# Two memory pools move below the weight pools in a two-layer decoder trunk

## The chip, the cores and the metric

The kernel runs on one core of one Trainium2 chip. The metric is the device time of one execution in microseconds (us). Before the change the median of three runs is 618.76 us (618.07 to 618.80). TensorE is called PE, VectorE DVE, ScalarE ACT, GpSimd POOL, SyncE SP. The on-chip memory has 128 partitions; "address" below means the byte within a partition at which a tile begins, the same in all partitions.

## The reference

The input is x, 256 tokens by 1024 features in float32. Two residual layers follow one another, each a mixer of sixteen attention heads and a gated feed-forward part:

```python
h = rms_norm(x, ev_norm)                       # layer 0
mixed = even_mixer(h, w_in, ...)               # 8 forgetting heads, 8 stick-breaking heads, 64 wide
x = x + mixed @ ev_w_out                       # 1024 x 1024
g, u = split(rms_norm(x, ffn_norm[0]) @ w_gate_up, 2)   # 1024 x 5632
x = x + (silu(g) * u) @ w_down                 # 2816 x 1024
h = rms_norm(x, od_norm)                       # layer 1
mixed = odd_mixer(h, w_in, ...)                # 8 block-sparse heads with a bias, 8 latent heads
x = x + mixed @ od_w_out
# ... and the same gated part with the second weights
```

All is float32. The weights, some 100 MB in all, are read once.

## The kernel before

**Products.** A float32 product a·b is made of three faster ones: each operand is split into a rounded high part and the rest, and hi·hi, hi·lo and lo·hi are summed in an accumulator `acc`. For weights ACT writes the high part `whi` (L244) and DVE the rest `wlo` (L252); for the normed input the parts are `xh`, `xl`, for the heads' outputs `oh`, `ol`, for the feed-forward's hidden values `hh`, `hl`, for the latent rows `lath`, `latl`. In a product one operand is *stationary* (128 by 128, loaded into PE by LDWEIGHTS) and the other *moving* (128 by 256, 384, 416 or 512 columns, streamed through). In nearly all the stationary operand is a piece of `xh`, `xl`, `oh`, `ol`, `hh`, `hl`, `lath` or `latl` (the two token halves, 128 columns each) and the moving one a row block of `whi` or `wlo`. For the projections of the stick-breaking heads it is the other way round: `whi` or `wlo` is stationary and `xh` or `xl` moves (L593).

**Stages.** Input projections and attention of layer 0 (to about 118 us), output projection (to 134 us), gate-up products of the feed-forward (134 to 262 us; eleven pairs of 48 products, 512 columns wide), down products (262 to 320 us), then the same for layer 1: latent projection, 416 columns wide (320 to 330 us), mixer (to 427 us), output projection, gate-up (442 to 556 us), down products (to 613 us). In the last half of the last down products one token half is split into two blocks of 256 columns, so products of 512 and 256 columns alternate there.

**Weights.** SP loads pieces of up to 1 MB into four buffers `raw` (L203 to L221); a new load is issued when DVE has made the last piece of an older one. The split pieces are made ahead of their use by a planned clock (L256); that clock counts columns and knows no addresses. Buffers: four `raw`, three `whi`, three `wlo`, 8192 bytes per partition each.

**Memory.** Each pool takes a stretch of addresses; pools are stacked in the order in which they are opened (L288 to L293, then L425 and later), and every tile takes a multiple of 32 bytes. `const` holds constants, `xpool` the residual stream, `wraw` the raw weights, `wsp` the split weights, `actp` the tiles `xh`, `xl`, `oh`, `ol` (32 tiles of 1024 bytes), `small` squares, factors and other small rows. Above them stands a pool for one attention layer (`att0`, `att1`), which makes room for the feed-forward's pool (`ffn0`, `ffn1`, with `hh`, `hl`) and back. `const` holds one tile of 32 bytes that nothing uses (L452).

**Order.** A scheduler sets the order of each engine's instructions from priorities and from the clock above. PSUM has four accumulators and four other banks.

The addresses at which the tiles begin, and what is left of them on division by 256:

| tiles | address before | mod 256 | mod 512 |
|---|---|---|---|
| `raw` (4) | 44288, then every 8192 | 0 | 256 |
| `whi` (3) | 77312, ... | 0 | 0 |
| `wlo` (3) | 101888, ... | 0 | 0 |
| `xh`, `xl`, `oh`, `ol` | 126464 to 159232, every 1024 | 0 | 0 |
| `small` | 159232 to 166784 | | |
| `hh`, `hl` | 179072, 181120, ... every 2048 | 128 | 384 |
| `lath`, `latl` | 182656, ... every 1024 | 128 | 384 |
| `mob` (bias rows, loaded by POOL's queue) | 170880 | 128 | 384 |

Within a tile the pieces used begin at multiples of 512 bytes (token halves) or of the row block's length: 2048 bytes for 512 columns, 1024 for 256, 1664 for 416. So of the 416-wide row blocks every second begins at 128 mod 256 and the others at 0.

Of the kernel before, what the change touches and what calls it, by code (L numbers as in the profile page):

```python
# [281 lines left out]
def trunk_kernel(ctx: ExitStack, tc: tile.TileContext, x, ffn_norm, w_gate_up, w_down, rel_bias,  # L282
# [4 lines left out]
    nc = tc.nc  # L287
    const = ctx.enter_context(tc.tile_pool(name="const", bufs=1))  # L288
    xpool = ctx.enter_context(tc.tile_pool(name="xpool", bufs=2))
    wraw = ctx.enter_context(tc.tile_pool(name="wraw", bufs=4))  # L290
    wsp = ctx.enter_context(tc.tile_pool(name="wsp", bufs=3))
    actp = ctx.enter_context(tc.tile_pool(name="actp", bufs=2))
    small = ctx.enter_context(tc.tile_pool(name="small", bufs=2))  # L293
    psA = ctx.enter_context(tc.tile_pool(name="psA", bufs=4, space=bass.MemoryType.PSUM))
    psB = ctx.enter_context(tc.tile_pool(name="psB", bufs=4, space=bass.MemoryType.PSUM))
    dram = ctx.enter_context(tc.tile_pool(name="dram", bufs=1, space=bass.MemoryType.DRAM))
# [1205 lines left out]
```

## Time and profile before

| | |
|---|---|
| median of three runs | 618.76 us (618.07 to 618.80) |
| the profiled execution | 618.59 us; its span, first to last instruction, 616.6 us |
| granted clock of TensorE | 0.999 of 2.4 GHz |
| busy in the span | PE 607.8 us, DVE 397.1, ACT 334.0, POOL 20.1 |
| read from HBM | 104.41 MB, 174 GB/s over the span |

A busy PE is not a PE at its best: products follow each other at a distance of their own, and a product's recorded time includes some of the next one's. The distance between the starts of two products, read from the timeline, is what counts; where the timeline has two products in one row ("x2"), two distances lie between that row's start and the next one's.

### The profile page before, as it was taken

Reading aid. Unit: us, or ns where it says so; the run is one execution under the profiler, and the core shown is the slowest. Engines: PE = TensorE matmul, PEld = TensorE weight load, DVE = VectorE, ACT = ScalarE, POOL = GpSimd, SP = SyncE. Lnnn points to the kernel's source line nnn. Section 1 sums busy time; section 2 is a strip of 40 time slices with the busy share of each in tenths; the row PEclk is TensorE's granted clock in tenths of the full one; section 3 lists DMA queues with packets and bytes.
Section 4 is the critical chain, followed back from the end, with each engine's and each line's share of the span. In section 5 each row is a group of like instructions: output and inputs, shape, how many; then the busy total and the mean of one; then the engine's idle time right before and its main releaser. Section 6 shows DMA issues by size and latency. Waiting matters only on the chain.

```text
span 616.6 us, 8999 instructions
## 1 busy us (share of the span) xinstructions
PE 607.8 (99%) x3398; PEld 513.9 (83%) x3398; DVE 397.1 (64%) x847; ACT 334.0 (54%) x693; POOL 20.1 (3%) x50
## 2 busy tenths in 40 slices
PE   8999999999999999999999999999999999999997
PEld 7988898778888888888889988777888888888896
DVE  4898777476655655745446797976656665664541
ACT  6856666464544554535357676966544454453430
POOL 7200000010000000000000000000000000000000
PEclk9999999999999999999999999999999999999999
DMA  8954443449645645565558344054465465465400
GB/s 254 370 175 137 142 144 127 137 138 286 234 162 176 228 144 191 185 205 167 180 174 266 129 137 138 17 189 138 136 218 192 146 225 175 157 218 201 179 32 35
DMA packets 84204, 106.07 MB, mean 172 GB/s; under 512 B 3532, under 2 KB 69394, under 8 KB 84032
## 3 DMA queue, kind: packets, MB, share of 16 engines
q1 hardware_dynamic: 82880, 101.49, 49.7%
q0 software_dynamic: 1120, 3.86, 1.9%
q8 instruction: 27, 0.44, 0.3%
q14 instruction: 17, 0.14, 0.1%
q10 hardware_dynamic: 160, 0.14, 0.1%
HBM read 104.41 MB, written 3.17 MB: 174 GB/s over the span
## 4 chain that ended last, share of the span: by engine, by line
PE 87%; DVE 5%; DMA 3%; ACT 3%; issue 1%; SPq 1%; DVEq 0%; POOLq 0%; ACTq 0%
PE acc L113 77%; PE ps L113 10%; DVE wlo L113 2%; DMA raw<-in_ev_w_in 1%; ACT whi L113 1%; DMA x<-in_x 1%; DMA cbc<-cd 1%; DVE sm L113 1%; DMA cd<-cum 1%; DVE m L113 0%; DVE pm L113 0%; ACT pm L113 0%; SPq L438 0%; DVE qkn L113 0%; ACT sqh L113 0%
## 5 line engine op out<-in xcount | busy, mean ns | idle before, releaser
L113 DVE TENSOR_TENSOR wlo<-raw,whi 128x512 fp32r<-128x512 f32 (+3 forms) x300 | 236.4, 826 | 93.4 <-ACT whi L113 92.8
L113 ACT ACTIVATE whi<-raw 128x512 fp32r<-128x512 f32 (+3 forms) x300 | 204.6, 740 | 96.0 <-PE acc L113 92.0
L113 PE MATMUL acc<-whi,xh 128*128 128x512 f32 (+3 forms) x592 | 179.9, 355 | 0.0
L113 PE MATMUL acc<-whi,xl 128*128 128x512 f32 (+3 forms) x592 | 177.2, 350 | 0.0
L113 PE MATMUL acc<-wlo,xh 128*128 128x512 f32 (+3 forms) x592 | 177.1, 349 | 0.0
L113 PEld LDWEIGHTS acc<-whi,xl 128*128 128x128 f32 x592 | 111.8, 189 | 15.0 <-issue 1.0
L113 PEld LDWEIGHTS acc<-wlo,xh 128*128 128x128 f32 x592 | 111.9, 189 | 14.2 <-DVE wlo L113 0.2
L113 PEld LDWEIGHTS acc<-whi,xh 128*128 128x128 f32 x592 | 110.1, 189 | 13.9 <-issue 1.3
L113 PE MATMUL acc<-whi,hl 128*128 128x512 f32 (+1 forms) x198 | 60.5, 370 | 0.0
L113 PE MATMUL acc<-whi,hh 128*128 128x512 f32 (+1 forms) x198 | 60.4, 370 | 0.0
L113 PE MATMUL acc<-wlo,hh 128*128 128x512 f32 (+1 forms) x198 | 60.0, 369 | 0.0
L113 ACT ACTIVATE sg<-acc,rs 128x256 f32<-128x256 f32 x44 | 18.5, 471 | 69.0 <-PE acc L113 65.7
L113 DVE SCALAR_TENSOR_TENSOR t<-acc,rs,sg 128x256 f32<-128x256 f32 x44 | 19.3, 479 | 50.7 <-ACT sg L113 50.7
L113 PEld LDWEIGHTS acc<-wlo,hh 128*128 128x128 f32 x198 | 35.8, 188 | 6.8
L113 PEld LDWEIGHTS acc<-whi,hl 128*128 128x128 f32 x198 | 35.9, 188 | 6.7
L113 PEld LDWEIGHTS acc<-whi,hh 128*128 128x128 f32 x198 | 35.6, 188 | 6.7
L113 ACT ACTIVATE hh<-ps 128x512 fp32r<-128x512 f32 x22 | 13.2, 599 | 42.4 <-PE ps L113 42.4
L113 DVE TENSOR_TENSOR hl<-ps,hh 128x512 fp32r<-128x512 f32 x22 | 15.2, 692 | 20.4 <-ACT hh L113 20.4
L113 ACT ACTIVATE pm<-lg,sm 128x128 f32<-128x128 f32 (+1 forms) x48 | 21.4, 455 | 9.0 <-DVE sm L113 8.9
L113 PE MATMUL acc<-whi,oh 128*128 128x512 f32 x64 | 22.2, 410 | 0.0
L113 PE MATMUL acc<-wlo,oh 128*128 128x512 f32 x64 | 21.2, 400 | 0.0
L113 PE MATMUL acc<-whi,ol 128*128 128x512 f32 x64 | 20.3, 394 | 0.0
(179 smaller groups left out, 587.1 us busy)
## 6 DMA issues: line engine op xcount, KB each, us to landing
raw<-in_ffn_w_gate_up SPq DMA_DIRECT2D x44, 1024.0 KB, 5.8
raw<-in_ffn_w_down SPq DMA_DIRECT2D x20, 1024.0 KB, 4.9
raw<-in_ev_w_in SPq DMA_DIRECT2D x10, 1024.0 KB, 6.9
raw<-in_od_w_in SPq DMA_DIRECT2D x6, 1024.0 KB, 5.2
raw<-in_ev_w_out SPq DMA_DIRECT2D x4, 1024.0 KB, 4.8
raw<-in_od_w_out SPq DMA_DIRECT2D x4, 1024.0 KB, 4.8
brep<-bd POOLq DMA_DIRECT2D x1, 2048.0 KB, 9.1
raw<-in_ffn_w_down SPq DMA_DIRECT2D x4, 512.0 KB, 3.7
```

What stands on the lines that cost most here:

```text
L113: r = f(*a, **k)
```

## The change

The pools `actp` and `small` are opened before `wraw` and `wsp` instead of after them:

```diff
     xpool = ctx.enter_context(tc.tile_pool(name="xpool", bufs=2))
+    actp = ctx.enter_context(tc.tile_pool(name="actp", bufs=2))
+    small = ctx.enter_context(tc.tile_pool(name="small", bufs=2))
     wraw = ctx.enter_context(tc.tile_pool(name="wraw", bufs=4))
     wsp = ctx.enter_context(tc.tile_pool(name="wsp", bufs=3))
-    actp = ctx.enter_context(tc.tile_pool(name="actp", bufs=2))
-    small = ctx.enter_context(tc.tile_pool(name="small", bufs=2))
```

`raw`, `whi` and `wlo` go up by 40320 bytes (157 times 256, and 128 more); the tiles of `actp` and `small` go down by 82176 bytes (321 times 256). All other tiles stay where they were, the attention and feed-forward pools too, since the four pools together are as long as before. The instructions of every engine, their order and their waits are the same; in the built program the addresses differ and nothing else.

| tiles | address after | mod 256 | mod 512 |
|---|---|---|---|
| `xh`, `xl`, `oh`, `ol` | 44288 to 77056 | 0 | 256 |
| `small` | 77056 to 84608 | | |
| `raw` (4) | 84608, ... | 128 | 128 |
| `whi` (3) | 117632, ... | 128 | 384 |
| `wlo` (3) | 142208, ... | 128 | 384 |
| `hh`, `hl`, `lath`, `latl`, `mob` | as before | 128 | 384 |

## Rows read from the trace of the kernel before

**Rows 1.** The page: span, busy time and share of each engine.
```profile
span 616.6 us, 8999 instructions
PE 607.8 (99%) x3398; PEld 513.9 (83%) x3398; DVE 397.1 (64%) x847; ACT 334.0 (54%) x693; POOL 20.1 (3%) x50
```

**Rows 2.** The page: the chain that ended last, by engine.
```profile
PE 87%; DVE 5%; DMA 3%; ACT 3%; issue 1%; SPq 1%; DVEq 0%; POOLq 0%; ACTq 0%
```

**Rows 3.** Busy time by stretch: start:end, length, engines, clock, DMA share, GB/s.
```profile
14.00:29.00 15.00, 15.00 (x124) 14.59 (x123) 12.21 (x38) 13.84 (x36) 4.47 (x9) 1.00 1.08 371
...
147.00:262.00 115.00, 115.00 (x529) 95.10 (x528) 71.05 (x97) 55.44 (x78) 0.00 (x0) 1.00 0.58 195
```

**Rows 4.** Timeline of PE, gate-up: start, us, operation.
```profile
200.22 0.62 PE L113 MATMUL acc<-whi,xh 128*128 128x512 f32 x2
...
202.94 0.62 PE L113 MATMUL acc<-whi,xh 128*128 128x512 f32 x2
```

**Rows 5.** Timeline of PE, output projection of layer 0.
```profile
121.34 0.62 PE L113 MATMUL acc<-whi,oh 128*128 128x512 f32 x2
...
123.61 0.61 PE L113 MATMUL acc<-whi,ol 128*128 128x512 f32 x2
```

**Rows 6.** Timeline of PE, down products of layer 0, both halves.
```profile
274.25 0.63 PE L113 MATMUL acc<-whi,hh 128*128 128x512 f32 x2
...
276.58 0.63 PE L113 MATMUL acc<-whi,hl 128*128 128x512 f32 x2
...
305.93 0.63 PE L113 MATMUL acc<-whi,hh 128*128 128x512 f32 x2
...
308.72 0.62 PE L113 MATMUL acc<-whi,hh 128*128 128x512 f32 x2
```

**Rows 7.** Timeline of PE, last down products, 512 and 256 columns in turn.
```profile
586.24 0.28 PE L113 MATMUL acc<-whi,hh 128*128 128x256 f32 x1
...
587.64 0.28 PE L113 MATMUL acc<-whi,hh 128*128 128x256 f32 x1
```

**Rows 8.** Timeline of PE, latent projection, 416 columns.
```profile
326.46 0.54 PE L113 MATMUL acc<-whi,xh 128*128 128x416 f32 x2
...
327.59 0.53 PE L113 MATMUL acc<-whi,xh 128*128 128x416 f32 x2
...
328.72 0.54 PE L113 MATMUL acc<-whi,xh 128*128 128x416 f32 x2
```

**Rows 9.** Timeline of PE, a projection of layer 0, 256 columns.
```profile
19.73 0.28 PE L113 MATMUL acc<-whi,xl 128*128 128x256 f32 x1
...
20.93 0.28 PE L113 MATMUL acc<-whi,xh 128*128 128x256 f32 x1
```

**Rows 10.** PE's groups by shape: operation, count, busy us, mean ns, idle.
```profile
L113 PE MATMUL acc<-whi,xh 128*128 128x512 f32 x352 | 110.6, 395 | 0.0
...
L113 PE MATMUL acc<-whi,xh 128*128 128x256 f32 x208 | 60.2, 290 | 0.0
...
L113 PE MATMUL acc<-whi,hl 128*128 128x512 f32 x154 | 51.5, 396 | 0.0
...
L113 PE MATMUL acc<-whi,oh 128*128 128x512 f32 x64 | 22.2, 410 | 0.0
...
L113 PE MATMUL acc<-xh,whi 128*128 128x256 f32 x64 | 19.1, 299 | 0.0
```

**Rows 11.** DVE's groups by shape: a target at 0, then one at 128.
```profile
L113 DVE TENSOR_TENSOR wlo<-raw,whi 128x512 fp32r<-128x512 f32 x190 | 122.5, 684 | 53.5 <-ACT whi L113 53.3
...
L113 DVE TENSOR_TENSOR qkn<-acc,sm 128x512 f32<-128x512 f32 x8 | 5.5, 685 | 0.3
```

**Rows 12.** Waits over the run: who for whom, us, times, longest.
```profile
ACT whi L113 <- DMA raw<-in_ev_w_in: 1.9, 2, 1.0
```

**Rows 13.** The page: the weights' DMA queue, packets, MB, share of 16 engines.
```profile
q1 hardware_dynamic: 82880, 101.49, 49.7%
```

**Rows 14.** DMA queues from 320 to 329 us: the queue that loads `mob`.
```profile
q0 software_dynamic: 272, 1.05, 32.2%
```

## The prediction

> **What bounds the kernel now.** Read in this order: the busy times, the chain that ended last, the stretches, and then, because the first three leave only one engine, the distances between products in PE's timeline. PE is busy 99% of the span [rows 1] and 87% of the chain [rows 2]; over the 115 us of gate-up it is busy 115.00 us, while DVE has 71.05, ACT 55.44 and the DMA engines a share of 0.58 [rows 3]. So a stretch gets longer or shorter only if PE's products follow each other at another distance, or if something slower than PE appears.
>
> The distances are where the reader must look closely, since the same product of 512 columns takes two values. Gate-up: from 200.22 to 202.94 us lie 12 products, 226.7 ns each [rows 4]. Output projection: from 121.34 to 123.61 lie 10, 227.0 ns [rows 5]. Down: 10 products from 274.25 to 276.58, 233.0 ns, and 12 from 305.93 to 308.72, 232.5 ns [rows 6]. The columns, the number of stationary columns, the accumulators and the `whi`/`wlo` buffers are alike, and the output projection's weights come in pieces of 512 columns as the down weights do. What differs is where the stationary tile lies: `xh`, `xl`, `oh`, `ol` begin at 0 mod 256, as `whi` and `wlo` do; `hh` and `hl` begin at 128. The excess is 232.75 - 226.7 = about 6.0 ns, 2.7%. So PE's pace does hang on addresses, or on something that goes with them, and this change alters nothing but addresses.
>
> **The change part by part.** Nothing is added, removed or put in another order, on SP's and POOL's queues either, and no wait is added. What changes is mod 256: `raw`, `whi`, `wlo` go from 0 to 128; `xh`, `xl`, `oh`, `ol` stay at 0; `hh`, `hl`, `lath`, `latl` stay at 128. Before, the two operands of a product stand alike in gate-up and the output projections and unlike in the down products; afterwards it is the reverse.
>
> *512 columns, operands that come to stand unlike.* The groups by shape give 352 for one of three products with `xh` and 64 for one of three with `oh` [rows 10]: 3 x (352 + 64) = 1248. No row of before has the moving operand at 128 and the stationary one at 0 at this width. The bounds: nothing, from the latent projection, whose six products on a row block at 128 take 1.13 us (326.46 to 327.59) and whose next six, on a block at 0, take 1.13 us as well [rows 8]; or 6.0 ns, from the down rows [rows 6]. I take 6.0, the row of the same width: 416 columns are 1664 bytes, so one end of each latent block stands off 256 either way and the pair is no clean test. 1248 x 6.0 ns = 7.5 us, ends 0 and 7.5.
>
> *512 columns, operands that come to stand alike.* 154 x 3 = 462 products with `hh` or `hl` [rows 10], of which 66 are in the last half where 512 and 256 columns alternate. There, nine products (three of 512, six of 256) take 1.40 us [rows 7], and by the distances of gate-up and of a 256-wide projection, 120 ns [rows 9], they would take 3 x 226.7 + 6 x 120 = 1400 ns: no excess to win. The other 396 may win 6.0 ns: -2.4 us, ends -2.4 and 0.
>
> *256 columns.* 3 x (208 + 64) = 816 products, in 192 of them the weights are stationary [rows 10]. Their distance is 120 ns now [rows 9]. Bounds from the rows above: the mixed stretch, where six 256-wide products unlike in place cost nothing [rows 7], or half of the 512-wide excess, 3.0 ns (2.4 us). I take 0, the row of the same width; the ends are 0 and +2.4 us. The few 264-, 384- and 416-wide products, some 120, go the same way and are under 0.5 us.
>
> *DVE and ACT.* They write and read at other places, but a DVE result at 128 takes 685 ns for 512 columns and one at 0 takes 684 [rows 11]: nothing, and what it could be is covered by PE, since DVE is free 38% of gate-up [rows 3].
>
> *The loads.* `raw` moves to 128 mod 256. The bias rows `mob` are loaded to an address at 128 already: 1.05 MB take 32.2% of 16 engines for 9 us, 46.4 us of engine time or 44 us per MB [rows 14]; the weights at 0 take 49.7% of 16 x 616.6 us for 101.49 MB, 48 us per MB [rows 13]. So no price shows; I take 0. What would be exposed are the first 30 us, where the DMA engines are saturated (share 1.08, 371 GB/s) [rows 3]; ACT waits 1.9 us for them now, in two waits [rows 12]. In the feed-forward the share of 0.58 is cover enough. A rule speaks against this part: the Trainium skill, "DMA: Bandwidth & Descriptors", section "How a descriptor splits into AXI transactions", has a descriptor that doesn't start at a multiple of 256 bytes begin at the boundary below and pay for the bytes before. It says so of reads; if it held for writes into the on-chip memory too, a 1024-byte row would pay 1152 bytes' worth, by my estimate from that page 12.5% more in the saturated 15 us, +1.9 us at most. The `mob` row disagrees, and the sum goes without it.
>
> *Sum.* 7.5 - 2.4 + 0 = +5.1 us on the profiled execution's own 618.59 us (span 616.6 and 2 us around it): 623.7 us. That execution is 0.17 us below the median of the three runs, which is less than a measurement of this kernel can tell (about 0.2%, 1.2 us).
>
> **The rivals.**
> *A, each operand pays for itself:* a product slows when either operand is off 256. Then gate-up pays 7.5 us and the down products win nothing: 626.1 us, up to 628.5 with the 256-wide. For it: the down rows fit it as well as they fit "unlike". Against: the latent blocks at 128 and 0 read the same.
>
> *B, the place of the moving operand doesn't matter,* only that of the stationary one, or the feed-forward tiles' region. All 512-wide stationary tiles keep their remainder; only the 192 products with stationary weights could change, within 0.6 us. 618.6 us. For it: the latent projection, six products at 1.13 us twice [rows 8]. Against: half of it is untested, since before no 512-wide product had its moving operand off 256; whether remainder or region slows `hh`, no row tells. The Trainium skill, "SBUF — State Buffer", section "Who interferes with whom", goes further: PE's reads of the moving and of the stationary operand are independent and PE waits on nobody, by which no address should matter and the time stays at 618.6; the two values of the distance in rows 4 and 6 are hard to square with it.
>
> *C, faster:* the slow case is only a stationary tile at 128 against a moving one at 0, and the opposite case is free, as in the latent rows. Then the down products win 2.4 us and gate-up pays nothing: 616.2 us. It decides against my forecast as soon as the 1248 products pay less than 2.4 us / 1248 = 1.9 ns each.
>
> *D, the loads pay* after all, in the first 30 us, with B otherwise: the two waits of 1.9 us double, 620.5 us.
>
> **How the numbers follow.** Forecast 0.42, A 0.12, B 0.20, C 0.20, D 0.06. Faster by over 0.2%: C, 0.20. Slower by over 0.2%: forecast, A and D, 0.60, less some small sizes of the forecast's excess (half of it gives +1.4 us after the gain): 0.56. Within: 0.24. The range runs from just under C (616.0) to A with part of the 256-wide products (627.0); the forecast's own, with 3 to 6 ns per product and 0 to 2.4 us for the narrow ones, is 620 to 626.
>
> **What would show it.** Gate-up and output projections at about 233 ns per product (a pair of eleven 0.3 us longer, the eleven pairs of a layer 3.2 us), down products at about 227: the forecast. Both at 233: A. All as before: B. Gate-up at 227 and down at 227: C. The 256-wide projections tell their own price against 120 ns. For D the waits on `raw` in the first 30 us would grow while PE's distances stay. The forecast is wrong if gate-up keeps 226.7 ns.

## The result and the profile after

The changed kernel takes 623.34 us (median of 4 runs, 623.24 to 624.02) against 618.64 us (618.07 to 618.80): a ratio of 1.008, 95% interval 1.0062 to 1.0097. It is slower by 4.7 us; 623.7 was forecast. Of the executions behind the medians below, one of alike_again (3418.71 us) is left out.

The page of the changed kernel's profiled execution (624.02 us), to be held against [rows 1]: the busy times of DVE, ACT and POOL are within 0.8 us of before, PE's is 6.4 us longer (its weight loads', PEld, 2.3 us) with the same number of instructions.

```profile
span 622.1 us, 8999 instructions
PE 614.2 (99%) x3398; PEld 516.2 (83%) x3398; DVE 397.7 (64%) x847; ACT 334.8 (54%) x693; POOL 20.0 (3%) x50
```

Now the distances, as in [rows 4 to 7]. First the timeline of PE in gate-up: seven rows of two products lie between the two starts, so 14 distances in 3.27 us, 233.6 ns, where before there were 226.7.

```profile
200.30 0.63 PE L113 MATMUL acc<-whi,xh 128*128 128x512 f32 x2
...
203.57 0.63 PE L113 MATMUL acc<-wlo,xh 128*128 128x512 f32 x2
```

The same view of the output projection (10 distances in 2.31 us: 231 ns, before 227.0), of the down products (10 in 2.27 us: 227 ns, before 233), and of the last half, where three products of 512 and six of 256 columns take turns (nine in 1.42 us, before 1.40):

```profile
122.19 0.62 PE L113 MATMUL acc<-whi,ol 128*128 128x512 f32 x2
...
124.50 0.64 PE L113 MATMUL acc<-wlo,oh 128*128 128x512 f32 x2
...
278.08 0.62 PE L113 MATMUL acc<-whi,hh 128*128 128x512 f32 x2
...
280.35 0.62 PE L113 MATMUL acc<-whi,hl 128*128 128x512 f32 x2
...
590.24 0.51 PE L113 MATMUL acc<-whi,hh 128*128 128x512 f32 x2
...
591.66 0.51 PE L113 MATMUL acc<-whi,hh 128*128 128x512 f32 x2
```

Where products of 512 columns follow one another, what was fast has become slow and the reverse: the slow ones are again those whose two operands differ mod 256. The 256-wide products of the projections come to stand unlike and get a little faster: 12 distances in 1.42 us, 118.3 ns, where there were 120 [rows 9].

```profile
19.81 0.28 PE L113 MATMUL acc<-whi,xh 128*128 128x256 f32 x1
...
21.23 0.28 PE L113 MATMUL acc<-whi,xh 128*128 128x256 f32 x1
```

The stages, from the start of the first product of one stage to that of the next (both read in the timelines, in us):

| stage | before | after | |
|---|---|---|---|
| first 256-wide projection to the first gate-up product | 116.65 | 118.01 | +1.36 |
| gate-up, layer 0 (with the last part of the output projection) | 125.42 | 128.20 | +2.78 |
| down, layer 0 | 63.10 | 61.77 | -1.33 |
| latent projection and mixer of layer 1 | 105.52 | 105.46 | -0.06 |
| gate-up, layer 1 | 125.63 | 128.50 | +2.87 |
| down, layer 1, first half | 31.35 | 30.68 | -0.67 |
| down, layer 1, last half (512 and 256 in turn) | 30.36 | 30.86 | +0.50 |

The first line of the table isn't PE's pace alone. The busy times by stretch of the changed kernel (columns as in [rows 3]) show the loads at 338 GB/s between 14 and 29 us, where they were at 371, and a granted clock of 0.93 in the next stretch:

```profile
14.00:29.00 15.00, 14.91 (x122) 14.35 (x121) 11.03 (x30) 12.64 (x34) 4.42 (x9) 1.00 1.10 338
29.00:53.00 24.00, 22.43 (x174) 21.09 (x174) 23.30 (x89) 14.89 (x42) 1.12 (x2) 0.93 0.50 161
```

The waits of the first 53 us go with it: ACT waits for `raw` 3.1 us in four waits (before 1.9 in two, [rows 12]), the chain behind it is late, and PE sits idle 1.6 us at its end (0.3 us before). Right behind that idle time, from 34.1 us on, the records show a clock of 1.2 GHz for 3.4 us.

```profile
ACT whi L113 <- DMA raw<-in_ev_w_in: 3.1, 4, 1.8
...
PE ps L113 <- DVE sm L113: 1.6, 1, 1.6
```

Of the four executions only this profiled one has the fall of the clock: the three other runs took 623.24 to 623.36 us at a clock of 1.0. So the stages of the profiled executions differ by 5.45 us in all, and the medians by 4.7.

### The profile page after: what moved, and what is told of

Its sections match the earlier page's. It is cut to its first block, busy times and chain, and to the rows that moved or that the text cites. A ratio compares the mean times of both kernels' runs of the same rounds, so it can differ in the third digit from the quotient of the medians.

```text
span 622.1 us, 8999 instructions
## 1 busy us (share of the span) xinstructions
PE 614.2 (99%) x3398; PEld 516.2 (83%) x3398; DVE 397.7 (64%) x847; ACT 334.8 (54%) x693; POOL 20.0 (3%) x50
## 4 chain that ended last, share of the span: by engine, by line
PE 88%; DVE 5%; ACT 3%; DMA 2%; issue 1%; SPq 1%; ACTq 0%
PE acc L113 78%; PE ps L113 10%; DVE wlo L113 2%; DMA raw<-in_ev_w_in 1%; ACT whi L113 1%; DMA x<-in_x 1%; DVE sm L113 1%; DVE m L113 1%; DVE pm L113 0%; DVE lg L113 0%; ACT pm L113 0%; SPq L438 0%; ACT sqh L113 0%; ACT sq L113 0%; DVE qkn L113 0%
## 5 line engine op out<-in xcount | busy, mean ns | idle before, releaser
L113 PE MATMUL acc<-whi,xh 128*128 128x512 f32 (+3 forms) x592 | 181.8, 357 | 0.0
L113 PE MATMUL acc<-wlo,xh 128*128 128x512 f32 (+3 forms) x592 | 179.3, 353 | 0.1
L113 PE MATMUL acc<-whi,xl 128*128 128x512 f32 (+3 forms) x592 | 179.3, 353 | 0.0
```

What stands on the lines that cost most here:

```text
L113: r = f(*a, **k)
```

## The experiments

**Theory 1:** the distance between products follows from the difference of the two operands' addresses mod 256. **Theory 2:** the order of the pools matters in another way (which region, which neighbours). **Theory 3:** a load to an address off 256 is slower where the DMA engines are saturated. The first four kernels below run the same instructions in the same order; they differ in unused bytes, and alike_above has the pools in the order of before.

*alike_below*: the changed kernel with a gap that brings the weights, and with them the pools above, to 0 mod 256.

```diff
     small = ctx.enter_context(tc.tile_pool(name="small", bufs=2))
+    pada = ctx.enter_context(tc.tile_pool(name="pada", bufs=1)); pada.tile([P, 32], F32, name="gapa")
     wraw = ctx.enter_context(tc.tile_pool(name="wraw", bufs=4))
```

> The pools in the order of the changed kernel, with 128 unused bytes between small and wraw: raw, whi, wlo and the feed-forward's hh, hl all begin at 0 mod 256, as xh and xl do. Theory 1 (the difference of the two operands' remainders mod 256 sets the distance of products): gate-up 226.7 ns, down 227 ns, so the time is that of before less the 1.4 us that the down products won in the changed kernel, 617.2 us. Theory 2 (not the remainder but the order of the pools, that is which tiles lie below which): gate-up stays at 233 ns and the time at 623.3 us.

616.94 us (6 runs, 616.80 to 617.61); against before 0.9974 (0.9963 to 0.9986). The timeline of PE, gate-up and then down: 12 distances in 2.72 us and 10 in 2.27, 226.7 and 227 ns. 128 bytes take back the whole loss and win more; theory 2 forecast 233 ns and 623.3 us here, and falls.

```profile
199.96 0.62 PE L113 MATMUL acc<-whi,xh 128*128 128x512 f32 x2
...
202.68 0.62 PE L113 MATMUL acc<-whi,xh 128*128 128x512 f32 x2
...
280.40 0.62 PE L113 MATMUL acc<-whi,hh 128*128 128x512 f32 x2
...
282.67 0.62 PE L113 MATMUL acc<-whi,hl 128*128 128x512 f32 x2
```

*alike_above*: the same gap above `small` in the order of before, so that only the attention and feed-forward pools move.

```diff
     small = ctx.enter_context(tc.tile_pool(name="small", bufs=2))
+    pada = ctx.enter_context(tc.tile_pool(name="pada", bufs=1)); pada.tile([P, 32], F32, name="gapa")
     psA = ctx.enter_context(...)
```

> The pools in the order of the kernel before, with 128 unused bytes above small: only the attention and feed-forward pools move, hh and hl to 0 mod 256. Theory 1: down products at 227 instead of 233 ns, gate-up stays at 226.7, 617.2 us, the same as with the pools in the other order. Theory 2: nothing changes, 618.6 us.

617.06 us (7 runs), 0.9978 (0.9967 to 0.9990): the same as alike_below with the other order. Once the remainders agree, the order of the pools is worth nothing that these runs can tell.

*raw_off*: as alike_below, with the gap between `wraw` and `wsp`: only `raw` is at 128. *raw_even*: as the changed kernel, with 128 unused bytes below `wraw` and above it: `raw` alone is at 0.

```diff
 # raw_off
     wraw = ctx.enter_context(tc.tile_pool(name="wraw", bufs=4))
+    pada = ctx.enter_context(tc.tile_pool(name="pada", bufs=1)); pada.tile([P, 32], F32, name="gapa")
     wsp = ctx.enter_context(tc.tile_pool(name="wsp", bufs=3))
```

> As alike_below, but the 128 unused bytes lie between wraw and wsp, so only raw begins at 128 mod 256; every pair of operands in PE is alike. Theory 1 alone: as alike_below, 617.2 us. Theory 3 (a load to 128 mod 256 takes the DMA engines longer per packet where they are saturated, 338 instead of 371 GB/s between 14 and 29 us): PE's distances as in alike_below, the first 30 us late by 0.4 to 1.2 us, 617.6 to 618.4 us.

> As the changed kernel, but raw begins at 0 mod 256 while whi, wlo, hh and hl stay at 128 (128 unused bytes below wraw and 128 above it). Theory 1 alone: gate-up 233, down 227 ns, 623.3 us. With theory 3: the same distances, 371 GB/s between 14 and 29 us, 622.1 to 622.9 us.

raw_off takes 617.96 us (11 runs), 1.0 us more than alike_below on the same chip. The single runs tell two prices apart: in five of the eleven the granted clock was 0.996 or 0.997, median 618.73 us, and in the other six at least 0.999, median 617.73; alike_below's six all had 1.0. So the loads cost 0.8 us, and 1.0 us more where the clock falls. raw_even takes 622.58 us (5 runs, 622.05 to 622.80), 0.8 us less than the changed kernel, whose four runs (623.24 to 624.02) were taken at another time. Busy times of 14 to 29 us, raw_off first and raw_even behind it: the loads' rate, the last number, follows `raw` alone.

```profile
14.00:29.00 15.00, 14.94 (x123) 14.52 (x122) 10.61 (x29) 12.19 (x33) 4.41 (x9) 1.00 1.10 339
```

```profile
14.00:29.00 15.00, 15.00 (x126) 14.72 (x125) 12.33 (x40) 13.83 (x36) 4.22 (x9) 1.00 1.07 371
```

raw_off's profile has the wait of PE (2.0 us) and the fallen clock (0.93 from 29 to 53 us) too; in raw_even's the same wait is 0.4 us and the clock stays at 1.00.

```profile
PE ps L113 <- DVE sm L113: 2.0, 1, 2.0
```

*sweep*: the distance measured by itself, in one execution at a granted clock of 1.0. The core of this new kernel, shortened, is

```python
def group(n, m, s):                      # m, s in elements past a multiple of 256 bytes
    for kt in range(8):
        for w, h in ((whi, xh), (wlo, xh), (whi, xl)):
            for tok in range(2):
                nc.tensor.matmul(a[tok][:, :n], h[:, s + 256 * kt + 128 * tok:][:, :128],
                                 w[:, m + 512 * kt:][:, :n], start=..., stop=...)
```

> Leaves out the whole model: TensorE alone runs groups of 48 products like those of gate-up (eight row blocks, three products each, two token halves), and each group has its own remainders mod 256 of the moving (m) and the stationary (s) operand; the output is filled with ones. Theory 1 (the difference m - s mod 256 decides): 512 columns at m = s take 226.7 ns a product whatever m is (0, 32, 64, 128), m - s = 128 takes 233 both ways (m 128, s 0 and m 0, s 128), and m 256 or s 256 are like 0. Its grain isn't known: if only multiples of 256 count, every other difference is slow; if the grain is 128, then 32 and 64 are something between. Rival (each operand's own remainder): m = s = 128 would be slow too. Rival (mod 512): m 256, s 0 would be slow. 256 columns: 120 ns alike and 117 to 120 unlike, as the kernels' traces show; 384 columns: 173.3 ns alike (columns plus 32 cycles of 2.4 GHz) and some 175.5 at 128.

The timeline of PE, the first row of a group and that of the next; n, m and s (bytes) stand in the accumulator's name. A group has 48 products, so the difference of two starts divided by 48 is the distance.

```profile
38.58 0.39 PE L70 MATMUL n512m0s0x<-whi,xh 128*128 128x512 f32 x1
49.46 0.63 PE L70 MATMUL n512m32s0x<-whi,xh 128*128 128x512 f32 x2
60.67 0.40 PE L70 MATMUL n512m64s0x<-whi,xh 128*128 128x512 f32 x1
71.66 0.63 PE L70 MATMUL n512m96s0x<-whi,xh 128*128 128x512 f32 x2
82.88 0.40 PE L70 MATMUL n512m128s0x<-whi,xh 128*128 128x512 f32 x1
94.07 0.40 PE L70 MATMUL n512m160s0x<-whi,xh 128*128 128x512 f32 x1
105.31 0.62 PE L70 MATMUL n512m192s0x<-whi,xh 128*128 128x512 f32 x2
116.51 0.40 PE L70 MATMUL n512m224s0x<-whi,xh 128*128 128x512 f32 x1
...
161.32 0.63 PE L70 MATMUL n512m0s128x<-whi,xh 128*128 128x512 f32 x2
172.48 0.40 PE L70 MATMUL n512m0s160x<-whi,xh 128*128 128x512 f32 x1
183.68 0.40 PE L70 MATMUL n512m0s192x<-whi,xh 128*128 128x512 f32 x1
194.68 0.40 PE L70 MATMUL n512m0s224x<-whi,xh 128*128 128x512 f32 x1
205.87 0.39 PE L70 MATMUL n512m128s128x<-whi,xh 128*128 128x512 f32 x1
216.76 0.62 PE L70 MATMUL n512m64s64x<-whi,xh 128*128 128x512 f32 x2
...
249.77 0.40 PE L70 MATMUL n512m256s0x<-whi,xh 128*128 128x512 f32 x1
260.70 0.62 PE L70 MATMUL n512m0s256x<-whi,xh 128*128 128x512 f32 x2
...
282.77 0.39 PE L70 MATMUL n512m16s0x<-whi,xh 128*128 128x512 f32 x1
293.89 0.40 PE L70 MATMUL n256m0s0x<-whi,xh 128*128 128x256 f32 x2
299.64 0.40 PE L70 MATMUL n256m32s0x<-whi,xh 128*128 128x256 f32 x2
305.30 0.40 PE L70 MATMUL n256m64s0x<-whi,xh 128*128 128x256 f32 x2
310.96 0.40 PE L70 MATMUL n256m96s0x<-whi,xh 128*128 128x256 f32 x2
316.70 0.40 PE L70 MATMUL n256m128s0x<-whi,xh 128*128 128x256 f32 x2
322.40 0.40 PE L70 MATMUL n256m160s0x<-whi,xh 128*128 128x256 f32 x2
...
386.95 0.55 PE L70 MATMUL n416m0s0x<-whi,xh 128*128 128x416 f32 x2
...
396.00 0.33 PE L70 MATMUL n128m0s0x<-whi,xh 128*128 128x128 f32 x2
```

With 512 columns: alike 226.7 ns (10.88 us), 32 off 233.5, 64 off 229.0, 96 off 233.8, 128 off 233.1. The other operand moved: 128 off 232.5, 192 (which is a difference of 64 again) 229.2. Both moved by 128: 226.9. Moved by 256: 227.7. The moving one 192 off pays in full, 233.3, so 64 and 192 aren't alike. At 512 columns, then, only the difference counts, moving minus stationary, mod 256, and theory 1 holds in the strong form; its grain is not 128 but finer, since 16 bytes already cost 5 ns (231.7). With 256 columns the sign turns: alike 119.8 ns, 32 or 64 off 117.9, 96 off 119.6, 128 off, which is the changed kernel's case, 118.7.

*loads*: theory 3 by itself, in one execution. SP alone loads 84 pieces of 1 MB.

> Leaves out the whole model: SP alone loads 84 pieces of 1 MB as gate-up's, rows of 1024 bytes, into four buffers, twelve pieces each at the remainders 0, 0, 128, 64, 32, 192 and 0 mod 256; the output is filled with weights. Theory 3 in the strong form (a row that doesn't start at a multiple of 256 takes one more piece of 256 bytes on its way): all remainders but 0 slow alike, from some 370 to some 338 GB/s, a median packet of 51 instead of 46 ns. Rival (only halves of 256, or only parts of 64 bytes, count): 128 slow and 64 not, or 32 slower than 64. Rival (the price in the whole kernels came from the other traffic of the first 30 us): 128 as fast as 0.

Busy times by stretch (length, POOL, clock, DMA share, GB/s), of stretches with the remainder 0, then 128 and 64, then 64 and 32, then 32 and 192:

```profile
20.00:55.00 35.00, 0.00 (x0) 1.00 1.09 386
...
90.00:125.00 35.00, 0.00 (x0) 1.00 1.10 348
125.00:160.00 35.00, 0.00 (x0) 1.00 1.10 348
160.00:195.00 35.00, 0.00 (x0) 1.00 1.09 348
```

386 GB/s at a multiple of 256 and 348 at every other remainder tried. A packet of 1024 bytes takes 46.0 ns on average at 0 and 51.2 to 51.7 ns off it, 11 to 12% more, at 32 as at 192. In the whole kernels the price shows where the DMA engines are saturated: from 14 to 29 us the median packet of 1024 bytes takes 46 ns before and 51 in the changed kernel, over the whole run 46 in both.

*apart64*: can the turned sign be used? As alike_below, but the split weights of the 256-wide projections lie 64 bytes further within their buffers, while all 512-wide products stay alike.

```diff
-        t = t[:, :un["n"]]
+        c = 16 if un["shape"][1:] == (256,) else 0; t = t[:, c:c + un["n"]]
...
-                un[t] = self.split_pool.tile([P, 2048], R32, name=f"w{t}{u}", tag=f"w{t}", bufs=3)
+                un[t] = self.split_pool.tile([P, 2112], R32, name=f"w{t}{u}", tag=f"w{t}", bufs=3)
...
-            self.rbc = small.tile([P, 256], F32, name=nm("rbc"), tag="rbc")
+            self.rbc = small.tile([P, 256], F32, name=nm("rbc"), tag="rbc", bufs=1)
```

> As alike_below, but in the 256-wide projections the weights lie 64 bytes further, so their 816 products have operands 64 (624 of them) or 192 apart mod 256, while all 512-wide products stay alike. The split weights' buffers grow by 256 bytes each and a row of factors has one buffer instead of two to make room; the order of instructions is the same. Theory 1 with the sweep's numbers (256 columns: 120.0 ns alike, 117.8 ns at 64 or 192): 816 x 2.2 ns = 1.8 us less than alike_below, 615.2 us. Rival: between transposes and attention products the 256-wide ones are too often interrupted for the distance to settle, or the stretch waits for attention anyway: 0 to 0.5 us less, 616.5 to 617 us.

> alike_below once more, on the chip of apart64, to compare it with: 616.9 us by every theory.

615.90 us (5 runs, 615.17 to 616.32), 0.9954 (0.9943 to 0.9966) against before; alike_again on the same chip 617.16 us (eight runs, 616.06 to 617.92), 0.9977 (0.9967 to 0.9987). The gain of 1.3 us lies between the 1.8 of the sweep, 615.2 us, and the 0.5 of the rival. The timeline of PE in a 256-wide projection: 10 distances in 1.18 us, 118 ns instead of 120 [rows 9].

```profile
19.50 0.28 PE L113 MATMUL acc<-whi,xh 128*128 128x256 f32 x1
...
20.68 0.28 PE L113 MATMUL acc<-wlo,xh 128*128 128x256 f32 x1
```

The products with stationary weights, whose operands stand 192 apart here, gain more: 10 distances in 1.14 us, 114 ns, where alike_below has 120. The sweep's group at 192, in which the moving operand was moved, has 117.8. So at 256 columns the difference alone does not give the pace; what else does was not tried.

```profile
57.15 0.28 PE L113 MATMUL acc<-xh,wlo 128*128 128x256 f32 x1
...
58.29 0.28 PE L113 MATMUL acc<-xh,whi 128*128 128x256 f32 x1
```

apart64 is the fastest version tried, 2.6 us under the median of before on its own chip (618.52 us). The single buffer for the row of factors was changed with it and not tried apart.

## Why the prediction was right, step by step

- *The step that carried it* (two distances for the same product in [rows 4 to 6], put down to unlike remainders) is shown for 512-wide products in a row by every kernel: about 227 ns alike and 231 to 234 at 128 apart, whichever operand is moved. Rival A (each operand pays for itself) falls with the down products at 227 ns with both at 128, B (nothing, or the stationary place alone) and C (only one direction) with gate-up at 233.
- *512 columns, unlike: mis-sized.* 7.5 us were put down. The two gate-up stages lost 2.78 + 2.87 = 5.65 us, 5.4 ns for each of 1056 products: every block of 48 begins with some irregular distances behind four transposes, and those hardly change (the first eight average 241 ns before and 242 after). The 192 products of the output projections pay 4 ns (231 against 227.0), 0.8 us, but the latent and mixer stage of layer 1, which holds half of them, did not get longer, since its 256-wide products get faster by 1 to 2 ns each as they come to stand unlike. That no price showed at 416 columns was no proof for 512. The reason given there, that a block of 1664 bytes stands off 256 at one end either way, is not shown: the sweep's 416-wide group, in which every block begins at 0, has 188.5 ns (386.95 to 396.00), the latent blocks 188.3 at either remainder [rows 8].
- *512 columns, alike:* -2.4 us put down, -1.33 - 0.67 = -2.00 measured on those 396 products.
- *The last half: wrong.* It was put at no change, since 1.40 us for nine is what three fast 512-wide and six 256-wide products at 120 ns make; three slow 512-wide ones at 233 and six fast 256-wide ones at 118 make it too, within 0.01 us. It lost 0.50 us, and neither reading forecasts that: by the sweep's distances it would have won a little. Read product by product in the traces, the 60 512-wide products that a 256-wide one follows take 236.2 ns alike where they took 231.7 unlike, and the 60 256-wide ones in front of a 512-wide one 119.1 where they took 115.8. So the rule of the sweep, whose groups have one width each, does not hold where widths alternate; alike_below and alike_above show the same, and why is not shown.
- *256 columns:* the value taken, 0, was the lower end of its range, and the sweep shows a gain of 1.1 to 1.3 ns at 128 apart (118.5 to 118.7 against 119.8), some 1 us for the 816 products by estimate from it. The range of that term should have reached below nothing.
- *The loads: wrong.* They were costed at nothing on the strength of `mob`; they cost about 0.8 us (raw_even against the changed kernel, raw_off's runs at full clock against alike_below), by rival D's mechanism. `mob`'s row could not show the price: its packets have 4096 bytes and were held against a queue whose packets mostly have 1024, and 44 and 48 us per MB are means over stretches of different load. The rule that was set aside, the Trainium skill, "DMA: Bandwidth & Descriptors", "How a descriptor splits into AXI transactions", is stated for reads. That a start off 256 costs is so here for writes into the on-chip memory too, but not by that page's count: by estimate from its sizes a row of 1024 bytes would take 3% more at 32, 6% at 64, 12.5% at 128 and 19% at 192, and the runs have 11 to 12% at all four.
- *The sum:* 5.65 - 2.00 + 0.50 + 0.8 = +4.95 us; the 0.8 us of the output projections and the gain of some 1 us of the 256-wide products nearly cancel, and 4.7 were measured between the medians. That +5.1 came so close is luck: the 512-wide terms were too large by some 1 us and 0.4 us with opposite signs, the 256-wide gain was left out, and the missed losses of 0.8 us in the loads and 0.5 in the last half filled what was left.
- *The other rule that was weighed,* that PE's two reads are independent (the Trainium skill, "SBUF — State Buffer", "Who interferes with whom"), is hard to square with the measurement: the same 48 products take 10.88 or 11.19 us by nothing but the two addresses.

What stays open is why. The runs show a law for 512-wide products in a row (the difference mod 256, with a grain finer than 64) and a weaker tendency the other way at 256, but not the mechanism, and other data types or stationary shapes were not tried. The fallen clock goes with the late loads: 5 of 11 executions of raw_off had it, none of alike_below's six. That it came from PE's idle 1.6 to 2.0 us right before it is the order of the rows, and was not tried apart.

## What to carry to other kernels

Where TensorE is the bound, look at the distance between products of one shape in several stages: if it takes two values, compare the two operands' addresses before looking for waits, and shift one by a gap of unused bytes. Give the loads' targets multiples of 256 bytes. Try the gap on the whole kernel: at 256 columns and where widths alternate, unlike operands were the faster here. A change of pools, their order or a tile's size shifts everything above it, so a small time that seems to come from such a change should be checked against a gap that restores the remainders.

## What the runs showed of the hardware that was not expected

- At 256 columns unlike operands are as fast or faster, 117.9 (32 or 64 apart) against 119.8 ns, and at 512 a difference of 64 costs 2.3 ns, a difference of 16 5.0, and the other multiples of 32 tried 5.8 to 7.1.
- Alike, 512-wide products settle at 226.7 ns and 256-wide ones at 120.0 [rows 4, 9], which is columns plus 32 cycles at 2.4 GHz in both; the sweep's 416-wide group, alike, takes 188.5, 1.8 ns more than that.
- Loads of 1024-byte rows to a start off 256 lose the same 10% of the rate (348 of 386 GB/s) at 32, 64, 128 and 192.
- One and the same 128 bytes moved the loads of the first 30 us (371 to 338 GB/s) and PE's pace for the rest of the time.
